# Late output-projection tiles: residual row loaded before the reciprocals, whose loads GpSimd issues

## The chip, the cores and the metric

The kernel runs on one core of a Trainium2 chip. The metric is the device time of one execution in microseconds (us); smaller is better. A core has five engines that work side by side, each through its own queue in order: TensorE (PE: matmuls and transposes, with its weight loads shown apart as PEld), VectorE (DVE), ScalarE (ACT), GpSimd (POOL) and SyncE (SP, which here only issues DMAs). POOL can issue DMAs too. An engine's instruction starts when the semaphores that it waits for have been raised by other engines or by DMAs that have landed.

## The reference

One step of a hybrid transformer with 1024 latent and 256 context tokens, D = 1024, two layers and a final RMSNorm. Layer 0 is gated attention with two mixers (A attends to all keys, B to a window with a sink logit), layer 1 is a Fourier mixer. The part around the change is the end of layer 0 and the beginning of layer 1:

```python
    # layer 0 (even), latents; the context tokens in the same way
    oa = dense_block_attention(qa, jnp.concatenate([ka, ka_ctx], axis=1), ...)
    ob = window_attention_with_ctx(qb, kb, vb, kb_ctx, vb_ctx, sink)
    yl = jnp.concatenate([oa * jax.nn.silu(ga), ob * jax.nn.silu(gb)], axis=-1) @ w_out
    xl = xl + gtl[:, None] * yl
    # layer 1 (odd)
    hl = modulate(rms_norm(xl, norm_g[l]), shl[:, None], scl[:, None])
    u, gate = jnp.split(hl @ w_in, 2, axis=-1)
    yl = (fourier_mix(u) * jax.nn.silu(gate)) @ w_out
```

## The kernel before

The tokens are ten tiles of 128 rows, r = 0 to 9 (8 and 9 are the context). All products of layer weights are made by `mm3` (L258): every float32 operand is split into a high and a low half in the PE's rounded float32 form, and a product is three matmuls (high by high, high by low, low by high; L265). A projection tile of 128x1024 outputs has two halves of 512 columns, 24 matmuls each.

**What is staged.** Attention runs in two sweeps over units (tile, head group, pair). `weigh` (L1040) makes the weighted values of a unit in PSUM (L1056); ACT copies its upper half out (L1065), DVE adds the lower half to it (L1067), and SP stores the result to `od` in DRAM (L1073). When a query tile is done, `totals` (L1021) takes the reciprocals of its softmax sums, transposes them (L1032), copies the row out on ACT (L1035), and SP stores it to `scd` in DRAM (L1037). The copies and sums of 64x256 and the rows of 16x128 share one pool of buffers, "e"; a buffer is free for its next user when the store that reads it has landed. The gates lie in `gd`.

**The output projection** is a filler: `proj_step` (L1325) of a tile is fed in between attention units, as soon as what it reads is finished, and the rest is drained when attention has ended (L1453). `proj_load` (L1316) calls `proj_in` (L1215), which loads a tile one or two tiles ahead (`load_to`, L1405):

- `ol`, the attention rows, from `od` (L1220), and `gl`, the gates, from `gd` (L1223);
- `rl`, the reciprocals, from `scd`: two loads, one for each mixer, each one row spread over 64 partitions (L1225, 64x1024, 256 KB);
- gates by reciprocals (L1226), by attention rows (L1227), both on POOL, and the split into high (L279) and low (L283) half;
- `xr`, the residual row, from the input (L1237), 128x1024.

`out_proj` (L1240) then makes both halves `oz` on PE, multiplies each by the layer's gate (L1248, DVE) and adds it to the residual row (L1249, DVE). `proj_step` stores the new row to `x1d` (L1348), squares it on ACT for the norm (L1349), and, when both tiles of a pair are done, makes 1/rms (`rsqrt`, with its power on POOL at L244), the pair's sum and difference (L1361 on ACT, L1362 and L1363 on DVE) and, with every second pair, four sums and differences of these (L1378, L1379, L1382, L1385, on DVE, with copies of one row on ACT). `quad_T` (L1279) transposes them on PE (`eoE`, `eoO`) for layer 1, between the halves of later tiles.

The pairs are (0,4), (2,6), (3,7), (1,5), (8,9), taken in that order. Tiles 0, 4, 2 and 6 are **early**: their loads are issued by POOL while attention runs (`ld`, L1216). Tiles 3, 7, 1, 5, 8 and 9 are **late**: attention's units have all been written (`late[0]`, L1451), and `ld` is SP. Their buffers come from the big zones `BIG` (`OB[0]`), handed out by `take` and returned by `drop`, and their PSUM banks from `next_bank` (L181), which goes round a ring of banks that includes the one in which the attention outputs are summed.

**What sets the order.** The kernel's text gives dependences and the sequence in which buffers are taken; a list scheduler with its own cost estimates then sets the order of each engine's queue, over the whole program. An edit in one place can so change the order on all engines from there on. DMAs issued by SP go round eight completion semaphores; a DMA waits for the one eight before it.

**Names in the orders below.** `oz_10502`/`oz_10530` are the halves of tile 7, `oz_10428`/`oz_10456` of tile 3, `oz_10666`/`oz_10694` of tile 5, `oz_10592`/`oz_10620` of tile 1. `av_30_10247` and `av_31_10267` are the last two attention units, whose sums are `e_10261` and `e_10281`; `e_10231` is the sum of the unit before, `e_10296` the last row of reciprocals. `p_10398` is the half of pair (2,6) that ACT makes, and `p_10403` the first of the four sums made from pairs (0,4) and (2,6); the three `eoE` transposes read it.

Of the kernel before, what the change touches and what calls it, by code (L numbers as in the profile page):

```python
# [17 lines left out]
P = 128  # L18
D = 1024
# [120 lines left out]
def hybrid_step(ctx: ExitStack, tc: tile.TileContext, I, O):  # L140
    nc = tc.nc
    pe, act, dve, pool, sp = nc.tensor, nc.scalar, nc.vector, nc.gpsimd, nc.sync
# [13 lines left out]
    def take(tag, shape, dt=F32):  # L156
        tags = (tag,) if isinstance(tag, str) else tag
        z = min((t for t in tags if spare[t]), key=lambda t: spare[t][0])
        i = spare[z].popleft()[1]
        size = 2 if dt == BF16 else 4  # L160
        for s in shape[1:]:
            size *= s
        assert size <= 4 * ZONES[z][1]
        made[0] += 1
        return Buf(z, i, up.tile(list(shape), dt, tag=f"{z}{i}", name=f"{z}{made[0]}", bufs=1))

    def drop(*bufs):
        for b in bufs:
            stamp[0] += 1
            spare[b.zone].append((stamp[0], b.idx))  # L170
# [22 lines left out]
    scd = dr.tile([NT, 2, 8, P], F32, name="scd")  # L193
# [76 lines left out]
    def pick(key, cycle):  # L270
        turn[key] = turn.get(key, -1) + 1
        return {"d": dve, "p": pool, "a": act}[cycle[turn[key] % len(cycle)]]
# [8 lines left out]
    def split(dst_h, dst_l, src, hc="a", lc="p"):  # L281
        copy("hi" + hc, hc, dst_h, src)
        pick("lo" + lc, lc).tensor_sub(dst_l, src, dst_h)  # L283
# [798 lines left out]
    def flush_held(n=0):  # L1082
        while len(held) > n:
            held.popleft()()
# [108 lines left out]
    OB, late = [("u", "w")], [False]  # L1193
# [21 lines left out]
    def proj_in(src, gate, r, resid):  # L1215
        ld = sp if gate is None or late[0] else pool  # L1216
        if gate is not None:
            flush_held()
            ol = take(OB[0], (P, 8, P))
            ld.dma_start(ol.a, src[r])  # L1220
            gl = take(OB[0], (P, 8, P))
            rl = take(OB[0], (P, 8, P))
            ld.dma_start(gl.a, gate[r])  # L1223
            for h in range(2):
                ld.dma_start(rl[64 * h : 64 * h + 64], scd[r, h].partition_broadcast(64))  # L1225
            pick("pm", XE["pm"]).tensor_mul(gl.a, gl.a, rl.a)  # L1226
            pick("pm", XE["pm"]).tensor_mul(ol.a, ol.a, gl.a)  # L1227
            drop(gl, rl)
        hi, lo = take(OB[0], (P, 8, P), F32R), take(OB[0], (P, 8, P), F32R)
        if gate is not None:  # L1230
            split(hi.a, lo.a, ol.a, "p" if late[0] else E_OH, E_OL)
            drop(ol)
        else:
            for c in range(2):
                split(hi[:, 4 * c : 4 * c + 4, :], lo[:, 4 * c : 4 * c + 4, :], src(c, r), "a", "d")
        xr = take(OB[0], (P, D))
        ld.dma_start(xr.a, resid[r * P : (r + 1) * P, :])  # L1237
        return hi, lo, xr

    def out_proj(name, r, ins, wo, gt, between=lambda h: None):  # L1240
        hi, lo, xr = ins
        for h in range(2):
            sl = slice(h * 512, h * 512 + 512)
            acc = next_bank(f"{name}{r}{h}") if late[0] else bank("g", f"{name}{r}{h}")
            mm3(acc, [(hi[:, k, :], lo[:, k, :], wo[k][0][:, sl], wo[k][1][:, sl]) for k in range(8)])
            between(h)
            yt = take("h", (P, 512))
            dve.tensor_mul(yt.a, acc, gt[:, sl])  # L1248
            pick("xa", XE["xa"]).tensor_add(xr[:, sl], xr[:, sl], yt.a)  # L1249
            drop(yt)  # L1250
        drop(hi, lo)
        return xr
# [63 lines left out]
    def proj_load(i, j):  # L1316
        r = pairs[i][j]
        v = r // 8
        if v not in gt0:
            gt0[v] = take(OB[0], (P, D))  # L1320
            sp.dma_start(gt0[v].a, gtd[0, v].partition_broadcast(P))
        ins[r] = proj_in(od, gd, r, I["xp"])
        return 0
# [459 lines left out]
    for g in range(4):  # L1783
# [34 lines left out]
        for r in (8, 9):  # L1818
            if AT_C[r - 8] == g:
                first[r] = proj_in(m1_at, None, r, x1d)  # L1820
# [7 lines left out]
    for r in (8, 9, 0, 1, 2, 3, 4, 5, 6, 7):  # L1828
        v = r // 8
        if v not in gt1:  # L1830
            gt1[v] = take(BIG, (P, D))
            sp.dma_start(gt1[v].a, gtd[1, v].partition_broadcast(P))
        ins1 = first.pop(r) if r in first else proj_in(m1_at, None, r, x1d)
        if r == 7:
            break
        xr = out_proj("of", r, ins1, wout1, gt1[v])
        yt = take(BIG, (P, D))
        ssq = sm.tile([P, 4], F32, tag="ssq", name=f"fss{r}")[:, 0:1]
        act.activation(yt.a, xr.a, AF.Square, accum_out=ssq)
        rs = rsqrt(f"frs{r}", ssq, 1, 1.0 / D, pw=PW[2])  # L1840
        dve.scalar_tensor_tensor(out=yt.a, in0=xr.a, scalar=rs[:, 0:1], in1=fg.a, op0=ALU.mult, op1=ALU.mult)
        sp.dma_start(O["y"][r * P : (r + 1) * P, :], yt.a)
        drop(xr, yt)


    hi, lo, xr = ins1
# [133 lines left out]
```

## Time and profile before

| what | us |
|---|---|
| median of 3 runs | 1191.29 |
| lowest and highest run | 1189.96, 1192.39 |
| the profiled execution | 1188.89 |
| its span, first to last instruction | 1187.1 |
| granted TensorE clock, mean of the span | 0.998 of full |

The page of the profile gives, for each engine, the time that it was busy, and groups of instructions by line. The timeline lists instructions in order of time: start, duration, engine, line, operation, output and inputs, count, and in brackets the idle time of the engine ahead of it with what ended it. A row with a count of several is a run of like instructions; matmuls overlap in the pipe, so that the distance between starts, not the printed duration, is what one costs. The tables of windows give each engine's busy time in a stretch, then the granted clock (PEclk), the busy share of the DMA engines and GB/s. The chain of waits goes back from the end of a stretch, at each step to what released it. Lines are those of the kernel before unless said otherwise; after the change the lines from L1225 on stand 3 or 4 higher.

### The profile page before, as it was taken

To read this page: it belongs to the slowest core of one execution; us is meant where nothing else is said; L and a number is where in the kernel's file an instruction comes from. 1 tells how busy PE (TensorE), PEld (TensorE's weight loads), DVE (VectorE), ACT (ScalarE), POOL (GpSimd) and SP (SyncE) were. 2 spreads that over 40 slices of the span, in tenths; PEclk is the share of its full clock that TensorE was granted. 3 is DMA by queue.
4 is the path that set the end of the run, shared out by engine and by line. 5 is a ranking of instruction groups with operands and counts; after the bars stand their busy time and mean duration, and the time that the engine had idled before them with its cause. 6 is when DMAs were issued, how large, how long until landed. Compare 5 with 4: busy or idle time off the path is not lost.

```text
span 1187.1 us, 22024 instructions
## 1 busy us (share of the span) xinstructions
PE 1150.7 (97%) x8103; PEld 1032.0 (87%) x8103; DVE 835.5 (70%) x1994; ACT 569.4 (48%) x1149; POOL 329.3 (28%) x294
## 2 busy tenths in 40 slices
PE   8999999999999999999999989999999999999997
PEld 6788899999999999899989887887877888998886
DVE  2489788877777776668888977876765962378543
ACT  4442455556656555556666674522363234342211
POOL 2355645512222221010110045275331226100001
PEclk9999999999999999999999999999999999999999
DMA  9978512323523232344352586785213426264321
GB/s 330 374 252 265 172 44 67 103 78 105 161 72 96 77 96 76 87 126 123 86 153 75 149 233 201 226 256 160 89 45 129 165 93 189 95 205 152 125 107 54
DMA packets 130096, 168.81 MB, mean 142 GB/s; under 512 B 26298, under 2 KB 86454, under 8 KB 129988
## 3 DMA queue, kind: packets, MB, share of 16 engines
q1 hardware_dynamic: 127476, 158.74, 43.4%
q0 software_dynamic: 2368, 8.39, 2.4%
q8 instruction: 64, 1.05, 0.4%
q14 instruction: 44, 0.36, 0.1%
q10 hardware_dynamic: 144, 0.26, 0.1%
HBM read 123.19 MB, written 44.16 MB: 141 GB/s over the span
## 4 chain that ended last, share of the span: by engine, by line
PE 76%; DMA 10%; DVE 6%; ACT 3%; issue 2%; SPq 2%; POOL 1%; POOLq 0%; DVEq 0%; ACTq 0%
PE of L265 9%; PE av L1056 9%; PE ga L265 8%; PE pt L1050 8%; PE q L265 8%; PE sL L933 5%; PE oz L265 4%; PE u L265 4%; PE g1O L265 4%; PE g1E L265 3%; PE kv L265 3%; PE sC L933 3%; PE g1c L265 2%; DMA od<-e 2%; DMA q<-qd 2%
## 5 line engine op out<-in xcount | busy, mean ns | idle before, releaser
L277 ACT ACTIVATE pt<-pt 128x512 fp32r<-128x512 f32 (+1 forms) x265 | 147.0, 576 | 107.6 <-PE pt L1050 60.3
L1053 DVE TENSOR_TENSOR pt<-pt,pt 128x512 fp32r<-128x512 f32 (+1 forms) x264 | 170.8, 658 | 37.9 <-ACT pt L277 37.0
L1056 PE MATMUL av<-pt,u 128*128 128x256 f32 x1008 | 167.0, 289 | 3.0 <-DVE e L1067 2.0
L1050 PE MATMUL pt<-identr,p 128*128 128x128 f32 x1008 | 156.9, 272 | 1.2 <-ACT p L974 0.8
L1056 PEld LDWEIGHTS av<-pt,u 128*128 128x128 f32 x1008 | 138.4, 189 | 7.1 <-DVE e L1067 2.6
L265 PE MATMUL q<-w,u 128*128 128x256 f32 x960 | 143.8, 287 | 0.0
L265 PEld LDWEIGHTS q<-w,u 128*128 128x128 f32 x960 | 126.9, 189 | 4.9 <-issue 0.8
L1050 PEld LDWEIGHTS pt<-identr,p 128*128 128x128 f32 x1008 | 119.3, 140 | 7.9 <-ACT p L974 1.0
L974 ACT ACTIVATE p<-p,nm 128x1280 f32<-128x1280 f32 (+1 forms) x80 | 95.5, 1194 | 62.3 <-DVE p L967 62.1
L265 PE MATMUL ga<-u,w 128*128 128x512 f32 (+1 forms) x576 | 124.4, 360 | 0.8 <-DVE byp L1029 0.5
L265 PEld LDWEIGHTS ga<-u,w 128*128 128x128 f32 x576 | 93.8, 188 | 15.0 <-ACT pt L277 1.2
L283 POOL TENSOR_TENSOR w<-h,w 128x512 fp32r<-128x512 f32 x38 | 51.1, 1363 | 143.5 <-DVE w L279 116.7
L933 PE MATMUL sL<-u,q 128*128 128x512 f32 x256 | 82.5, 411 | 1.4 <-DMA q<-qd 1.4
L974 ACT ACTIVATE p<-p,NM 128x640 f32<-128x640 f32 (+2 forms) x80 | 59.1, 739 | 38.1 <-DVE p L967 38.0
L933 PE MATMUL sC<-u,q 128*128 128x256 f32 x320 | 61.5, 293 | 2.3 <-DMA q<-qd 2.0
L967 DVE TENSOR_SCALAR_CACHE_REDUCE p<-sL 128x512 f32<-128x512 f32 x64 | 43.9, 685 | 23.5 <-PE sL L933 14.6
L967 DVE TENSOR_SCALAR_CACHE_REDUCE p<-sL,nm 128x512 f32<-128x512 f32 x64 | 47.7, 745 | 13.5 <-PE sL L933 12.6
L265 PE MATMUL oz<-u,w 128*128 128x512 f32 x192 | 56.9, 400 | 0.0
L707 POOL TENSOR_TENSOR h<-h,rope 128x512 f32<-128x512 f32 (+1 forms) x18 | 21.9, 1217 | 125.8 <-ACT h L790 80.0
L933 PEld LDWEIGHTS sC<-u,q 128*128 128x128 f32 x320 | 48.8, 189 | 6.4 <-DVE tot L1023 1.7
L265 PE MATMUL oz<-u,u 128*128 128x512 f32 x160 | 47.8, 402 | 4.3 <-DVE h L1248 2.4
L283 POOL TENSOR_TENSOR u<-h,u 128x512 fp32r<-128x512 f32 x16 | 21.1, 1325 | 108.6 <-ACT u L277 104.3
(728 smaller groups left out, 2590.1 us busy)
## 6 DMA issues: line engine op xcount, KB each, us to landing
q<-qd SPq DMA_DIRECT2D x80, 256.0 KB
h<-i_w_in SPq DMA_DIRECT2D x40, 256.0 KB
p<-i_ada_w SPq DMA_DIRECT2D x18, 512.0 KB
h<-i_w_out SPq DMA_DIRECT2D x32, 256.0 KB
pt<-i_ada_w SPq DMA_DIRECT2D x15, 512.0 KB
qd<-pt SPq DMA_DIRECT2D x20, 256.0 KB
q<-i_ada_w SPq DMA_DIRECT2D x9, 512.0 KB
qd<-q SPq DMA_DIRECT2D x18, 256.0 KB
```

The source lines that it names most:

```text
L265: pe.matmul(out, a, b, start=i == 0, stop=i == n - 1)
L277: act.activation(out, in_, AF.Copy)
L283: pick("lo" + lc, lc).tensor_sub(dst_l, src, dst_h)
L707: pick("rope", XE["rope"]).tensor_mul(t1.rearrange("p t h (b c) -> p t (h b) c", b=2), y.rearrange("p t h (b c) -> p t (h b) c", b=2), cb)
L933: pe.matmul(ps, q_at(q, s, hc), keys, start=s == 0, stop=s == 1)
L967: dve.tensor_scalar(p[i][:, end[i] : end[i] + n], ps, sign, last[i], op0=ALU.mult, op1=ALU.min, accum_out=c)
L974: act.activation(p[i][:, 0 : end[i]], p[i][:, 0 : end[i]], AF.Exp, bias=last[i], scale=-1.0, accum_out=SU[:, t, hd + i, 0:1],)
L1050: pe.transpose(tp[:, jj * 256 + i * P : jj * 256 + i * P + P], p[i][:, off : off + P], ident)
L1053: dve.tensor_sub(pt[:, 1, 0:n], tp[:, 0:n], pt[:, 0, 0:n])
L1056: pe.matmul(acc, vv, pt[:, s, jj * 256 : jj * 256 + 256], start=c + jj + s == 0, stop=c + jj == nt - 1 and s == 1,)
```

## The change

In `proj_in`, for tiles that are late, the residual row's buffer is taken, and its load issued by SP, right behind the load of the gates; the two loads of reciprocals are issued by POOL in place of SP. Early tiles have their loads in the order and on the queue that they had.

```diff
             gl = take(OB[0], (P, 8, P))
             rl = take(OB[0], (P, 8, P))
             ld.dma_start(gl.a, gate[r])
+            if late[0]:
+                xr = take(OB[0], (P, D))
+                sp.dma_start(xr.a, resid[r * P : (r + 1) * P, :])
             for h in range(2):
-                ld.dma_start(rl[64 * h : 64 * h + 64], scd[r, h].partition_broadcast(64))
+                pool.dma_start(rl[64 * h : 64 * h + 64], scd[r, h].partition_broadcast(64))
             pick("pm", XE["pm"]).tensor_mul(gl.a, gl.a, rl.a)
...
-        xr = take(OB[0], (P, D))
-        ld.dma_start(xr.a, resid[r * P : (r + 1) * P, :])
+        if gate is None or not late[0]:
+            xr = take(OB[0], (P, D))
+            ld.dma_start(xr.a, resid[r * P : (r + 1) * P, :])
         return hi, lo, xr
```

Six late tiles with two loads each: 12 DMA issues go from SP's queue to POOL's, and six loads of a residual row move ahead of the work on the gates. The buffers are taken in another sequence, too (tile 7's residual row is `pt_10328` before, `p_10320` now). No arithmetic is added or left out.

The scheduler's order is another one from there on. On PE, before, at the end of tile 7's second half and ahead of the first transposes, tile 5's first half stands around the last attention unit:

```order
L265 MATMUL oz_10530<-u_9276,q_10325 128x512
L265 MATMUL oz_10666<-u_8504,w_10496 128x512
L265 MATMUL oz_10666<-u_8505,w_10496 128x512
L1056 MATMUL av_31_10267<-pt_10273,u_7079 128x256 x4
L265 MATMUL oz_10666<-u_8504,u_10497 128x512
...
L265 MATMUL oz_10666<-u_9276,u_10497 128x512
L1279 MATMUL eoE_10820<-identr,p_10403 128x128
L1279 MATMUL eoE_10831<-identr,p_10403 128x128
L1279 MATMUL eoE_10844<-identr,p_10403 128x128
L265 MATMUL oz_10428<-u_8504,w_10309 128x512
```

And PE at the same place of the program now:

```order
L1056 MATMUL av_31_10267<-pt_10273,u_7079 128x256 x4
L265 MATMUL oz_10530<-u_8850,q_10326 128x512
...
L265 MATMUL oz_10530<-u_9276,pt_10327 128x512
L1283 MATMUL eoE_10820<-identr,p_10403 128x128
L1283 MATMUL eoE_10831<-identr,p_10403 128x128
L1283 MATMUL eoE_10844<-identr,p_10403 128x128
L265 MATMUL oz_10428<-u_8504,u_10311 128x512
...
L265 MATMUL oz_10428<-u_9276,w_10312 128x512
L265 MATMUL oz_10666<-u_8504,u_10498 128x512
```

The 24 matmuls of `oz_10666` stood between tile 7's last matmul and the transposes; they now stand behind the transposes and behind the 24 of `oz_10428`. The last attention unit stands 18 matmuls of tile 7 ahead of the transposes.

On ACT, the difference of the two orders around the last copies of attention (a row with - stands there before, with + now):

```order
 L1035 ACTIVATE e_10244<-tt_10242 16x128
+L1353 ACTIVATE h_10386,ss_104<-u_9925 128x1024
 L1065 ACTIVATE e_10230<-av_31_10217 64x256
-L1361 ACTIVATE p_10398<-u_9925,r11y 128x1024
+L1065 ACTIVATE e_10260<-av_30_10247 64x256
 L1035 ACTIVATE e_10296<-tt_10294 16x128
-L1065 ACTIVATE e_10260<-av_30_10247 64x256
+L1365 ACTIVATE p_10398<-u_9925,r11y 128x1024
 L1065 ACTIVATE e_10280<-av_31_10267 64x256
```

`p_10398` stood ahead of the last row of reciprocals (L1035) and now stands behind it; the copy of the last attention unit but one (L1065 `e_10260`) has moved ahead of both.

On SP, the difference around the store of the sum `e_10231`:

```order
-L1223 DMA q_10653<-gd 128x1024
-L1225 DMA u_10580<-scd 64x1024 x2
-L1237 DMA pt_10328<-i_xp 128x1024
-L1223 DMA u_10579<-gd 128x1024
+L1352 DMA x1d<-u_9925 128x1024
 L1073 DMA od<-e_10231 64x2x128
+L1226 DMA w_10492<-i_xp 128x1024
 L1037 DMA scd<-e_10296 16x127
```

Ahead of that store stood two loads of gates, two of reciprocals and tile 7's residual row; now there stands the store of tile 6's new row, and a residual row's load follows behind it.

## The prediction

> **What bounds the kernel now.** I read the page first, then the waits of PE in the stage that the change touches, then the chain of waits there, then the timelines of SP, DVE and ACT.
>
> ```profile
> span 1187.1 us, 22024 instructions
> PE 1150.7 (97%) x8103; PEld 1032.0 (87%) x8103; DVE 835.5 (70%) x1994; ACT 569.4 (48%) x1149; POOL 329.3 (28%) x294
> ```
>
> PE is busy for 97% of the span. An edit moves the end only by making PE's gaps shorter or longer, or its clock lower. The changed loads start at about 760 us (a row further below); the matmuls that use them, and the transposes behind them, lie between 783 and 880 us. There PE waits three times, of which two matter:
>
> ```profile
> PE oz L265 <- DVE u L283: 1.9, 1, 1.9
> PE av L1056 <- DVE e L1067: 1.0, 1, 1.0
> PE eoO L1279 <- DVE pt L1269: 0.3, 1, 0.3
> ```
>
> The two lie next to each other (PE's timeline: start, duration, instruction, count, idle time ahead with its releaser):
>
> ```profile
> 791.07 0.63 PE L1056 MATMUL av<-pt,u 128*128 128x256 f32 x4
> 791.54 0.27 PE L1032 MATMUL tt<-identr,byp 128*16 128x128 f32 x1
> ...
> 802.56 0.63 PE L265 MATMUL oz<-u,w 128*128 128x512 f32 x2
> 804.16 0.74 PE L1056 MATMUL av<-pt,u 128*128 128x256 f32 x4 [0.97 <-DVE e L1067]
> 806.77 0.79 PE L265 MATMUL oz<-u,u 128*128 128x512 f32 x1 [1.87 <-DVE u L283]
> ...
> 809.92 0.63 PE L265 MATMUL oz<-u,w 128*128 128x512 f32 x2
> ```
>
> The chain of waits (start, length, what) says whence the two waits come:
>
> ```profile
> 796.91 5.97 DMA od<-e
> ...
> 802.99 0.28 ACT e L1035
> ...
> 803.69 0.42 DVE e L1067
> 804.11 2.62 DVE u L283
> ...
> 813.58 0.33 PE eoE L1279 x3
> 813.91 11.11 PE oz L265 x48
> ```
>
> A store of an attention sum lands late; ACT's last row of reciprocals (L1035) waits for its buffer, and behind it in ACT's queue stands the copy that DVE's sum (L1067) needs.
>
> The gap has a tail, in the windows (us, busy time of PE, PEld, DVE, ACT and POOL, granted clock, DMA share, GB/s):
>
> ```profile
> 730.00:740.00 10.00, 7.55 (x41) 6.24 (x39) 9.90 (x24) 6.56 (x14) 5.48 (x6) 1.00 0.52 150
> 800.00:810.00 10.00, 7.16 (x26) 5.34 (x25) 8.20 (x8) 1.03 (x3) 4.69 (x4) 0.83 0.47 152
> ```
>
> The clock was 0.83 in that stretch. Seven matmuls start from 806.77 up to 809.92, so they took 3.15 us. At full clock one costs 0.23 (the chain's last row: 11.11 / 48 = 0.2315), seven 1.6: 1.5 lost. **The gap costs 0.97 + 1.87 + 1.5 = 4.35 us**, the most that the change can win here.
>
> Why did the store land late?
>
> ```profile
> 794.62 1.09 SPq L1225 DMA_DIRECT2D u<-scd  x2
> 795.81 0.54 SPq L1237 DMA_DIRECT2D pt<-i_xp  x1
> 796.43 0.39 SPq L1223 DMA_DIRECT2D u<-gd  x1
> 796.91 0.62 SPq L1073 DMA_DIRECT2D od<-e  x1
> ```
>
> ```profile
> 793.77 0.41 DVE L1067 TENSOR_TENSOR e<-av,e 64x256 f32<-64x256 f32 x1
> ...
> 801.53 0.69 DVE L1249 TENSOR_TENSOR pt<-pt,h 128x512 f32<-128x512 f32 x1 [4.12 <-DMA pt<-i_xp]
> 802.14 1.28 DVE L1362 SCALAR_TENSOR_TENSOR pt<-w,r11y,p 128x1024 f32<-128x1024 f32 x1
> ...
> 804.03 2.69 DVE L283 TENSOR_TENSOR u<-u,w 128x1024 fp32r<-128x1024 f32 x1
> 806.64 1.27 DVE L1363 SCALAR_TENSOR_TENSOR p<-w,r11y,p 128x1024 f32<-128x1024 f32 x1
> ...
> 812.08 0.41 DVE L1067 TENSOR_TENSOR e<-av,e 64x256 f32<-64x256 f32 x1
> 812.42 2.54 DVE L1249 TENSOR_TENSOR pt<-pt,h 128x512 f32<-128x512 f32 x1
> 814.88 1.21 DVE L1385 TENSOR_TENSOR p<-w,p 128x1024 f32<-128x1024 f32 x1
> ```
>
> The stored sum was ready at 793.77 + 0.41 = 794.18, but SP's queue held two loads of reciprocals, the residual row and a gate ahead of it: issued at 796.91. Just these issues the change takes away, and with them DVE's 4.12 us for the residual row.
>
> **The change part by part.** *What it takes off SP.* With only the store of tile 6's row ahead, which was ready long before, the store can go at about 794.3, 2.6 earlier. By the row's 5.97 it lands at 800.3. The residual row's wait of 4.12 ends 2.2 us before the other (802.22 against 804.11), so by itself it hardly moves PE; next behind it is ACT's L1035.
>
> *What it adds on POOL.*
>
> ```profile
> L1225 SPq DMA_DIRECT2D u<-scd x8: 450/480/590, 761.3 to 807.3; - x8
> L1225 POOL DMA_DIRECT2D u<-scd x4: 522/539/567, 695.3 to 737.7; - x4
> DMA to landing us min/median/max: 4.2/5.8/6.4
> DMA to landing us min/median/max: 3.6/8.0/11.8
> ```
>
> (The first landing line is that of the reciprocals, on either queue; the second that of the residual rows.) An issue costs 0.48 on SP and 0.54 on POOL: 12 x 0.48 = 5.8 us of SP's queue go, 12 x 0.54 = 6.5 us of POOL's come, 1.1 a tile. POOL's multiplies behind them start that much later. I cost this at nothing: tile 5's high half, which PE used at 802.56, is now used behind 24 matmuls of another tile, some 13 us later (sum below), and later tiles have more. Without that cover it is 1.1 us a tile, or what a late landing costs (rival C). The Trainium skill, page "SBUF — State Buffer", section "🔬 SBUF: two separate sides", speaks against this part: descriptors of a DMA issued from GpSimd's queue are written by GpSimd, which DVE can lock out, and a DMA of 620 ns took 3100. By that, as an estimate from the page, a load would be 2.5 us later, and with all of it on the path the time 2.5 us longer. The landings above, of loads from both queues, 4.2 to 6.4, show nothing of it.
>
> *What it moves.* PE's order loses the 24 matmuls of tile 5's first half ahead of the three transposes, 24 x 0.2315 = 5.6 us of cover. The transposes need the first quad sum (p_10403), and the 24 matmuls behind them a PSUM bank that the last attention sum (e_10281) empties. Both stand at the end of this chain: L1361, L1362, L1363, L1378, then e_10281. And ACT's part of it was early:
>
> ```profile
> 796.79 1.16 ACT L1361 ACTIVATE p<-u,r11y 128x1024 f32<-128x1024 f32 x1 [4.67 <-POOL r11y L244]
> 802.99 0.27 ACT L1035 ACTIVATE e<-tt 16x128 f32<-16x128 f32 x1 [5.04 <-DMA od<-e]
> ```
>
> Before, L1361 ran at 796.79, ahead of the row that waits for the store. Now it stands behind it. Two more rows, and then step by step:
>
> ```profile
> 814.99 1.06 ACT L1349 ACTIVATE h<-pt 128x1024 bf16<-128x1024 f32 x1 [2.88 <-DVE pt L1249]
> 732.89 2.33 PE L265 MATMUL oz<-u,u 128*128 128x512 f32 x9 [2.45 <-DVE h L1248]
> ```
>
> 1. PE has two matmuls of tile 5 less: after the row of 802.56 only the last attention unit's four (791.07 to 791.54: 0.47) remain to be placed earlier, so PE comes to the transposes at 802.56 + 0.47 = 803.03 and would be through at 803.36.
> 2. ACT: store landed at 800.3, L1035 0.27, L1361's successor from 800.6 to 801.8.
> 3. DVE: L1362 1.28, then the same six instructions as from 806.64 to 812.49: 5.85. e_10281 at 801.8 + 7.1 = 808.9.
> 4. A DVE operation with two inputs in SBUF that meets a multiply of POOL is stretched: the rows of 2.69 (1.21 for that shape in the row of 814.88) and 2.54 (0.69 in the row of 801.53) lose 1.5 and 1.85. Those six met none in their 5.85. It can now meet none to three of POOL's multiplies; I take one, 1.7, as in 804.03: e_10281 at 810.6.
> 5. PE stands idle for 810.6 - 803.36 = 7.2 us, in two pieces, at the transposes and at the half behind them. Should the last attention unit itself wait earlier, that comes off these pieces.
> 6. Then come 24 + 2 matmuls, 6.0 us, before tile 5's low half is needed. DVE has till then three operations of 0.69, two of 1.21 and ACT's square between (1.06): 5.55. No further wait; at the most the 1.87 of before.
>
> 7. The clock. The idle 2.84 of 803 to 807 cost 1.5 behind it; the idle 2.45 at 732.89 cost nothing (clock 1.00 in its window). A wait of 7.2 is beyond both; I take the nearer, 1.5, with 0 and two such tails, 3.0, as bounds. The Trainium skill, "TensorE: Matmul & The Clock Gate", gives half clock after an idle window of 3.4 us; with a wait of that length at each of two places it would be some 3.4 us of loss by the page, 1.9 more than my term, and no run here has yet shown a wait so long.
>
> **Sum**: 7.2 + 0 + 1.5 - 4.35 = +4.35 us. The profiled execution of 1188.89 would be 1193.2; it stands 2.4 below the median, and the difference on the median of 1191.29 gives **1195.6**. Nothing later gives it back: PE has no other wait but the one of 0.3 us until 880, and what follows is issued in PE's order.
>
> Bounds: the store could land as fast as the reciprocals' fastest load, 4.2; then, with no meeting and no tail, e_10281 is at 807.1 and the sum is 3.7 - 4.35 = -0.6. Upwards: three meetings (+3.4), the 1.87, two tails (+1.5): +11.1.
>
> **The rivals.**
>
> A. *The change does what it says*: the store, freed from SP's queue, lands within 2.4 us, and the chain is done before PE needs it. A store's landing is bounded below by this row of the chain at another place:
>
> ```profile
> 734.75 2.12 DMA scd<-e
> ```
>
> With 2.12 L1035 is through by 796.7, ACT's product is done at 798.0 (POOL's r11y of 796.79 is then as late), e_10281 at 805.1: idle 1.7, no tail, -2.6. With less, up to -4.35. That is **1186.9 to 1188.7**, faster. It decides as soon as the chain ends before 805.3. For it speaks that 2.7 of the store's lateness are SP's; against it that stores of this form took 5.97 here with the DMA engines half idle (0.47).
>
> B. *An equal wait takes the place of the one removed*: step 2 to 5 hold, but DVE meets no multiply and PE's clock does not fall. Then 5.5 - 4.35 = +1.2, and with a landing of 4.2 -0.6: **1190.7 to 1192.5**, no change. It decides where POOL's multiplies fall, which the issues on POOL move by 1.1 us a tile.
>
> C. *POOL's loads come late*: an issue on POOL waits, behind it its multiplies, and PE waits for tile 5's or tile 1's high half on top of the forecast. The worst landing of a residual row, 11.8, against the reciprocals' 5.8, is +6.0: with the sum **1201.6**. For it speaks that POOL's queue is in order, and that a load whose buffer is still in use holds all multiplies behind it; against it 4.2 to 6.4 in all landings so far.
>
> **How the numbers follow.** About 0.2%, 2.4 us, is what a measurement of this kernel can tell from no change. The forecast, slower by 2.4 to 11, gets 0.63: it rests on orders that are given, and on one stretched operation. A gets 0.12, B 0.17, C 0.08. So faster 0.12, same 0.17, slower 0.63 + 0.08 = 0.71. The range goes from B's and the bound's lower end, with a little of A, 1189.0, to the upper bound of the sum, 1191.29 + 11.1 = 1202.4; outside lie A and the worst of C, under 0.2.
>
> **What would show it.** In the changed kernel's timeline PE should wait at the transposes (L1283) for DVE's L1382 and at the next half for L1067, 7 us together, and the 0.97 and 1.87 should be gone. ACT's L1365 should start behind L1035 after 800 us. The store of e_10231 should be issued at about 794.3, and DVE should no longer wait for a residual row. The window of 800 to 820 should have a clock under 1. The prediction is wrong if the transposes wait for less than 2 us, if L1365 runs before 798, or if PE's waits are for POOL's halves (L279), not DVE's sums.

## The result, and the profile after

| | kernel before | changed kernel |
|---|---|---|
| median, us | 1190.93 (7 runs) | 1196.78 (7 runs) |
| lowest and highest run | 1187.80, 1192.39 | 1192.37, 1198.89 |
| ratio to the kernel before | | 1.0053, 95% interval 1.0038 to 1.0067 |
| span of the profiled execution | 1187.1 | 1192.6 |

The changed kernel is slower by 5.9 us; 4.35 were forecast, and the range holds the time. The waits of PE between 730 and 900 us are now two of a kind that the kernel before did not have:

```profile
PE eoE L1283 <- DVE p L1382: 4.8, 1, 4.8
PE oz L265 <- DVE e L1067: 3.6, 1, 3.6
```

PE's timeline shows them next to each other, at the three transposes and at tile 3's half behind them:

```profile
801.29 0.40 PE L265 MATMUL oz<-u,pt 128*128 128x512 f32 x1
806.50 0.90 PE L1283 MATMUL eoE<-identr,p 128*128 128x128 f32 x3 [4.81 <-DVE p L1382]
811.04 1.22 PE L265 MATMUL oz<-u,u 128*128 128x512 f32 x2 [3.64 <-DVE e L1067]
...
814.93 0.63 PE L265 MATMUL oz<-u,u 128*128 128x512 f32 x2
```

Together 8.45 us. And the clock stays low for longer than before (windows, columns as before; the last three are granted clock, DMA share, GB/s):

```profile
800.00:810.00 10.00, 2.59 (x11) 1.53 (x9) 10.00 (x5) 0.45 (x1) 8.44 (x7) 0.73 0.59 202
810.00:820.00 10.00, 8.96 (x31) 7.20 (x32) 8.11 (x11) 2.82 (x4) 4.75 (x3) 0.76 0.79 251
```

Nine matmuls start from 811.04 up to 814.93: 3.89 us where 9 x 0.2315 = 2.08 would do, 1.8 lost; the transposes took 0.90 for the 0.33 of before, 0.6 more. 8.45 + 1.8 + 0.6 - 4.35 of before = 6.5. That is 0.7 more than the stage measures below; 0.3 of it is the third wait of before (`eoO`), which is gone, and the rest isn't accounted for.

One profiled execution differs from the next in places that have nothing to do with the change, so a yardstick is needed that leaves them out. It is the length of the stage from the last transposes of reciprocals but one (L1032) to the first matmul of the context's part of layer 1 (`g1c`): up to a matmul or two it holds the same PE work in all kernels here. Before and after:

```profile
778.49 0.27 PE L1032 MATMUL tt<-identr,byp 128*16 128x128 f32 x1
...
889.05 0.50 PE L265 MATMUL g1c<-u,u 128*128 128x256 f32 x2 [0.44 <-ACT u L1268]
```

```profile
776.95 0.27 PE L1032 MATMUL tt<-identr,byp 128*16 128x128 f32 x1
...
893.28 0.50 PE L265 MATMUL g1c<-u,w 128*128 128x256 f32 x2 [0.44 <-ACT u L1272]
```

110.57 before, 116.33 after: +5.8, as much as the measured difference. Each is one execution. lock_probe (below) has the order of the kernel before up to the piece added behind it, and so gives that stage a second time: 111.23. What DVE did meanwhile:

```profile
789.00 0.42 DVE L1067 TENSOR_TENSOR e<-av,e 64x256 f32<-64x256 f32 x1 [0.89 <-ACT e L1065]
...
797.60 2.23 DVE L1366 SCALAR_TENSOR_TENSOR pt<-w,r11y,p 128x1024 f32<-128x1024 f32 x1 [2.34 <-ACT p L1365]
799.87 3.30 DVE L1367 SCALAR_TENSOR_TENSOR p<-w,r11y,p 128x1024 f32<-128x1024 f32 x1
803.09 3.36 DVE L1382 TENSOR_TENSOR p<-w,pt 128x1024 f32<-128x1024 f32 x1
...
806.97 2.55 DVE L1386 TENSOR_TENSOR pt<-w,p 128x1024 f32<-128x1024 f32 x1
...
810.58 0.41 DVE L1067 TENSOR_TENSOR e<-av,e 64x256 f32<-64x256 f32 x1
```

The chain that PE waits for starts at 797.60, earlier than forecast, and takes 13.4 us, longer than forecast: four of its operations last 11.4 us that took 1.28 + 1.27 + 1.21 + 1.45 = 5.2 before. GpSimd was at work beside each of them:

```profile
793.30 2.40 POOL L1229 TENSOR_TENSOR w<-w,q 128x1024 f32<-128x1024 f32 x1 [8.49 <-DMA w<-gd]
...
796.36 2.39 POOL L1229 TENSOR_TENSOR u<-u,u 128x1024 f32<-128x1024 f32 x1
798.72 3.37 POOL L1230 TENSOR_TENSOR u<-u,w 128x1024 f32<-128x1024 f32 x1
...
802.30 3.07 POOL L1230 TENSOR_TENSOR p<-p,u 128x1024 f32<-128x1024 f32 x1
...
806.41 1.05 POOL L279 CAST u<-u 128x1024 fp32r<-128x1024 f32 x1
807.39 1.05 POOL L279 CAST w<-p 128x1024 fp32r<-128x1024 f32 x1
```

The first of these rows says why its work lay there: GpSimd had stood still for 8.49 us, for a load of gates. SP issued that load at 783.32, and it landed 9.8 us later; why so late wasn't followed up.

ACT and SP, ahead of the chain:

```profile
794.43 0.38 ACT L1065 ACTIVATE e<-av 64x256 f32<-64x256 f32 x1 [5.47 <-DMA od<-e]
795.85 0.27 ACT L1035 ACTIVATE e<-tt 16x128 f32<-16x128 f32 x1 [1.04 <-DMA w<-i_xp]
796.41 1.15 ACT L1365 ACTIVATE p<-u,r11y 128x1024 f32<-128x1024 f32 x1 [0.29 <-POOL r11y L244]
```

```profile
789.44 0.58 SPq L1073 DMA_DIRECT2D od<-e  x1
```

The store of e_10231 goes out as soon as the sum is made (789.00 + 0.42), so SP's queue is no longer in its way, and DVE waits for no residual row. The change does what it says; what comes with it costs more. With the durations of before, the chain from 797.60 would have been done at 804.8, and PE, through with the transposes at 802.0, would have stood idle for some 2.8 us, about as long as the two waits that the change took away (0.97 + 1.87). This is an estimate, and no run tests it: none has the changed kernel's order without the longer operations.

### The profile page after: what moved, and what is told of

It reads as the page before. It is cut to its first block, busy times and chain, and to the rows that moved or that the text cites. A ratio compares the mean times of both kernels' runs of the same rounds, so it can differ in the third digit from the quotient of the medians.

```text
span 1192.6 us, 22027 instructions
## 1 busy us (share of the span) xinstructions
PE 1154.3 (97%) x8103; PEld 1035.5 (87%) x8103; DVE 840.2 (70%) x1994; ACT 570.2 (48%) x1149; POOL 336.2 (28%) x306
## 4 chain that ended last, share of the span: by engine, by line
PE 80%; DMA 7%; DVE 6%; issue 2%; ACT 2%; POOL 1%; SPq 1%; POOLq 0%; DVEq 0%; ACTq 0%
PE of L265 9%; PE ga L265 9%; PE av L1056 9%; PE pt L1050 8%; PE q L265 8%; PE oz L265 6%; PE sL L933 5%; PE u L265 4%; PE g1E L265 3%; PE g1O L265 3%; PE sC L933 3%; PE kv L265 3%; PE g1c L265 2%; DMA w<-gd 1%; PE sB L1005 1%
## 5 line engine op out<-in xcount | busy, mean ns | idle before, releaser
L283 POOL TENSOR_TENSOR w<-h,w 128x512 fp32r<-128x512 f32 x38 | 51.0, 1360 | 144.0 <-DVE w L279 117.2
L265 PE MATMUL oz<-u,u 128*128 128x512 f32 x224 | 63.6, 404 | 3.6 <-DVE e L1067 3.6
L967 DVE TENSOR_SCALAR_CACHE_REDUCE p<-sL,nm 128x512 f32<-128x512 f32 x64 | 47.7, 745 | 13.4 <-PE sL L933 12.5
L265 PEld LDWEIGHTS oz<-u,u 128*128 128x128 f32 x224 | 41.9, 192 | 13.1 <-DVE e L1067 4.0
L265 PE MATMUL oz<-u,w 128*128 128x512 f32 x176 | 52.9, 399 | 0.0
```

The lines of the kernel that those rows point to most:

```text
L265: pe.matmul(out, a, b, start=i == 0, stop=i == n - 1)
L967: dve.tensor_scalar(p[i][:, end[i] : end[i] + n], ps, sign, last[i], op0=ALU.mult, op1=ALU.min, accum_out=c)
```

## The experiments

Theories, as the expectations name them. **O**: the order counts; PE waits for what its new order puts next, and the queue on which a load is issued costs nothing. **D** is its sharper form: both waits stand at the end of one chain on DVE. **T**: the transposes stand too early, and that is all. **Q**: loads issued by GpSimd hold up its multiplies. **X**: the early residual rows cost. **L**: the reciprocals come sooner outside SP's queue, so that GpSimd's multiplies run beside DVE's chain. **K**: DVE and GpSimd shut each other out.

All kernels at a glance (ratio to the kernel before, measured alongside, with its interval; stage as above, from one profile of each kernel):

| kernel | residual row | reciprocals by | ratio (95%) | stage, us |
|---|---|---|---|---|
| before | last | SP | 1 | 110.57 |
| changed | early | GpSimd | 1.0053 (1.0038 to 1.0067) | 116.33 |
| xr_only | early | SP | 0.9979 (0.9964 to 0.9994) | 108.74 |
| pool_only | last | GpSimd | 1.0057 (1.0034 to 1.0079) | 115.34 |
| act_q | early | ScalarE | 0.9989 (0.9975 to 1.0003) | 107.58 |
| before_bare | last | SP | 1.0042 (1.0027 to 1.0058) | 114.84 |
| after_t81 | early | GpSimd | 1.0058 (1.0037 to 1.0079) | 116.34 |
| after_e | early | GpSimd | 1.0027 (1.0012 to 1.0043) | 113.91 |
| xr_e | early | SP | 0.9973 (0.9956 to 0.9991) | 108.92 |
| act_e | early | ScalarE | 0.9992 (0.9976 to 1.0009) | 110.33 |

**Each half of the change alone, and another queue.** xr_only is the changed kernel with

```diff
-                pool.dma_start(rl[64 * h : 64 * h + 64], scd[r, h].partition_broadcast(64))
+                ld.dma_start(rl[64 * h : 64 * h + 64], scd[r, h].partition_broadcast(64))
```

> One part alone: late residual rows are loaded early, the reciprocals' loads stay on SP. In its order the first transposes stand behind tile 8, 230 matmuls later than in the change. Theory O (PE waits for whatever DVE's chain its order puts next; the queue of the loads costs nothing): no wait at the transposes, a gap of at most the old 4.35 us, so 1187 to 1191 us and a ratio of 0.996 to 1.000. Theory Q (loads issued by GpSimd hold up its multiplies): no such loads, 1.000. Theory X (early residual rows cost, by their buffers and SP's queue): as slow as the change, 1.005.

Measured 1187.91 us, ratio 0.9979: faster, so X falls. There is no wait at the transposes; PE waits twice, as long as in the kernel before:

```profile
PE oz L265 <- DVE u L283: 1.9, 1, 1.9
PE av L1056 <- DVE e L1067: 0.9, 1, 0.9
```

pool_only is the kernel before with

```diff
-                ld.dma_start(rl[64 * h : 64 * h + 64], scd[r, h].partition_broadcast(64))
+                pool.dma_start(rl[64 * h : 64 * h + 64], scd[r, h].partition_broadcast(64))
```

> The other part alone: GpSimd issues the late reciprocals, the residual row is loaded last as before. In its order the transposes stand right behind tile 7's last matmul, as in the change. Theory O: PE waits at the transposes or at tile 3's half for the last attention sum, 3 us or more, ratio 1.002 to 1.006. Theory Q: 1.005, with waits of PE for GpSimd's halves. Theory X: 1.000.

Measured 1196.40 us, ratio 1.0057. This half alone gives all of the slowdown. Its waits and, on DVE, the longest operation of its chain:

```profile
PE eoE L1279 <- DVE p L1378: 3.0, 1, 3.0
PE oz L265 <- DVE e L1067: 2.8, 1, 2.8
PE av L1056 <- DVE e L1067: 1.4, 1, 1.4
```

```profile
804.91 4.77 DVE L1378 TENSOR_TENSOR p<-w,pt 128x1024 f32<-128x1024 f32 x1
```

PE waits for DVE's sums, as O has it; not once for a half that GpSimd makes, as Q would. act_q is the changed kernel with

```diff
-                pool.dma_start(rl[64 * h : 64 * h + 64], scd[r, h].partition_broadcast(64))
+                (act if late[0] else pool).dma_start(rl[64 * h : 64 * h + 64], scd[r, h].partition_broadcast(64))
```

> The change, but the late reciprocals are issued by ScalarE in place of GpSimd. PE's order from tile 7 on is that of xr_only, with the transposes behind tile 8. Theory O in its simple form: as xr_only, 0.996 to 1.000. Theory Q: as before, 1.000. Theory L (the reciprocals come sooner when they are not in SP's queue, so that GpSimd's multiplies run beside DVE's chain and stretch it): slow whatever PE's order, 1.003 to 1.006, with DVE operations of 2 to 3.4 us in the chain.

Measured 1189.01 us, ratio 0.9989. The waits:

```profile
PE oz L265 <- DVE pt L283: 1.3, 1, 1.3
PE oz L265 <- DVE u L283: 0.7, 1, 0.7
```

It too takes the reciprocals out of SP's queue, and is not slow. L forecast operations of 2 to 3.4 us in its chain, and they aren't there:

```profile
798.27 1.72 DVE L1366 SCALAR_TENSOR_TENSOR pt<-w,r11y,p 128x1024 f32<-128x1024 f32 x1
...
804.71 1.27 DVE L1367 SCALAR_TENSOR_TENSOR p<-w,r11y,p 128x1024 f32<-128x1024 f32 x1
805.91 1.22 DVE L1382 TENSOR_TENSOR p<-w,pt 128x1024 f32<-128x1024 f32 x1
```

So loads outside SP's queue don't by themselves bring GpSimd's work beside the chain, and this half of L falls. What a chain stretched by GpSimd costs, the other half, this run doesn't test. So far the slow kernels are those that have the transposes bare behind tile 7, and they are also those in which GpSimd issues; Q is not yet out.

**The order without the loads.** before_bare leaves every load where it was in the kernel before, and binds only PE's order:

```diff
+            if (r, h) == (5, 0):
+                for ins in mms[5, 0][:1]:
+                    tc.add_manual_dep(ins, mms[3, 0][-1].name, mybir.DependencyInfo(mybir.DependencyClass.NoSync, mybir.DependencyReason.SCHED_ONLY), reason="order")
```

(`mms[r, h]` are the matmuls of tile r's half h; an edge of this kind sets the order on PE and adds no wait. Up to 812 us the orders of DVE, ACT, GpSimd and SP are those of the kernel before.)

> The kernel before with all loads as they were; one constraint of order on PE alone puts tile 5's first half behind tile 3's, so that the transposes stand bare behind tile 7's last matmul, as in the change. Theory O: PE waits at the transposes for DVE's first quad sum and then for the last attention sum, 2 to 6 us more than before, ratio 1.002 to 1.005. Theories Q, X and L: the loads are those of before, 1.000.

Measured 1195.13 us, ratio 1.0042; O holds, Q, X and L would have had 1.000. PE waits

```profile
PE eoE L1283 <- DVE p L1382: 4.2, 1, 4.2
PE av L1057 <- DVE e L1068: 1.6, 1, 1.6
PE oz L265 <- DVE e L1068: 1.4, 1, 1.4
```

with no load moved. In this kernel the order alone costs 4.2 thousandths, 5 us. Its chain on DVE isn't stretched, but for a low half's L284 of 2.69 that stands in it as in the kernel before; it starts late, behind the wait for the residual row that the changed kernel no longer has:

```profile
804.15 0.69 DVE L1253 TENSOR_TENSOR pt<-pt,h 128x512 f32<-128x512 f32 x1 [4.24 <-DMA pt<-i_xp]
804.76 1.28 DVE L1366 SCALAR_TENSOR_TENSOR pt<-w,r11y,p 128x1024 f32<-128x1024 f32 x1
...
809.25 1.27 DVE L1367 SCALAR_TENSOR_TENSOR p<-w,r11y,p 128x1024 f32<-128x1024 f32 x1
810.45 1.21 DVE L1382 TENSOR_TENSOR p<-w,pt 128x1024 f32<-128x1024 f32 x1
```

So the same place of the transposes lays bare two different chains: here a late one of plain operations, in the changed kernel (and in pool_only) an early one that GpSimd stretches by some 6 us.

**Transposes, or DVE's chain?** after_t81 is the changed kernel in which PE's first transposes must come behind tile 8:

```diff
-            pe.transpose(tp[:, n * P : n * P + P], row[:, k * P : k * P + P], ident)
+            with tc.issue_after(ends[8, 1].ins) if key == "E" and k < 3 else nullcontext():
+                pe.transpose(tp[:, n * P : n * P + P], row[:, k * P : k * P + P], ident)
```

> The changed kernel with one constraint of order on PE: the first transposes come behind tile 8's last matmul. DVE's order up to the last attention sum (e_10281) is that of the change, with the chain of quad sums ahead of it. Theory D (PE waits for the end of DVE's chain, and tile 3's half waits there for the PSUM bank that e_10281 empties): the two waits of the change, 4.8 and 3.6 us, become one of 8 to 9.5 ahead of tile 3's half, and the time stays that of the change, ratio 1.004 to 1.006 to the kernel before. Theory T (the transposes stand too early, and that is all): their 4.8 us and part of the slow clock go, ratio 1.000 to 1.002.

Measured 1197.55 us, ratio 1.0058, and the stage as long as that of the changed kernel to 0.01 us, with the orders of DVE and GpSimd unchanged. T falls. The two waits have become one:

```profile
PE oz L265 <- DVE e L1068: 9.0, 1, 9.0
```

after_e leaves the transposes and puts the chain on DVE behind the last attention sum (`sums[-1]`):

```diff
-        dve.scalar_tensor_tensor(out=xe.a, in0=xa.a, scalar=rs[:, 0:1], in1=xo_.a, op0=ALU.mult, op1=ALU.add)
+        with tc.issue_after(sums[-1]) if i == 1 else nullcontext():
+            dve.scalar_tensor_tensor(out=xe.a, in0=xa.a, scalar=rs[:, 0:1], in1=xo_.a, op0=ALU.mult, op1=ALU.add)
```

> The changed kernel with one constraint of order on DVE: the last attention sum e_10281 comes ahead of the chain of quad sums. In its order tile 3's half follows tile 7's directly, then the transposes, then tile 5. Theory D: tile 3's half no longer waits, its 24 matmuls (5.6 us) run beside DVE's chain, and the transposes wait for less than 2 us; what is late next are tile 5's halves, whose high half GpSimd has ready at about 807.5 in the change and whose low half DVE makes behind its chain: 2 to 6 us of waiting there. Ratio 1.000 to 1.004, 1 to 6 us faster than the change. Theory T: the transposes still wait 4 us or more, with little change of the time, 1.004 to 1.006.

Measured 1193.93 us, ratio 1.0027: 2.4 us of the stage come back. The waits are as D foresaw, the next one being tile 5's low half, which DVE makes behind its chain:

```profile
PE oz L265 <- DVE u L283: 4.7, 1, 4.7
PE eoE L1284 <- DVE p L1384: 1.5, 1, 1.5
```

So it isn't one instruction that stands wrongly. DVE has some 13 us of work there, of which about 6 are the stretch, and what PE does meanwhile must not need it.

**Why the chain took 13 us.** lock_probe adds a piece behind the end of the kernel before, in which DVE and GpSimd run on buffers of their own: six additions alone, six beside four multiplies, eight from PSUM beside four multiplies, six beside four casts, four multiplies alone.

```diff
+            if name == "mul" or name == "psum":
+                pool.tensor_mul(go.a, ga_.a, gb_.a)
+            if name == "cast":
+                pool.tensor_copy(gr.a, ga_.a)
...
+            if name == "psum":
+                dve.tensor_add(vo[:, 0:512], vp, vb[:, 0:512])
+            else:
+                dve.tensor_add(vo.a, va.a, vb.a)
```

> The kernel before, with a piece added behind its end that measures one thing by itself: DVE additions of 128x1024 with both inputs in SBUF, first alone, then beside GpSimd multiplies of 128x1024, then 128x512 additions with one input in PSUM beside such multiplies, then the first kind beside GpSimd casts; at the end the multiplies alone. Theory K (the two engines shut each other out): alone 1.21 and 2.40; beside each other they take turns, so that the DVE operations that meet a multiply last 2 to 3.7 us and the multiplies beside them grow too, while the additions from PSUM keep 0.68 and the multiplies beside those 2.40. Rival (a shared bandwidth): every operation of both engines grows by one factor. Rival (no interplay; the long operations in the change have another cause): 1.21, 0.68 and 2.40 throughout.

Its time, 1252.98 us, is that of the added piece. The five parts as windows (us, then busy time and count of PE, PEld, DVE, ACT, POOL):

```profile
1195.30:1202.90 7.60, 0.00 (x0) 0.00 (x0) 7.35 (x6) 0.00 (x0) 0.00 (x0) 0.50 0.00 0
1202.90:1218.70 15.80, 0.00 (x0) 0.00 (x0) 15.44 (x6) 0.00 (x0) 13.00 (x4) 0.50 0.00 0
1218.70:1228.50 9.80, 0.00 (x0) 0.00 (x0) 5.53 (x8) 0.00 (x0) 9.39 (x4) 0.50 0.00 0
1228.50:1239.00 10.50, 0.00 (x0) 0.00 (x0) 10.22 (x6) 0.00 (x0) 7.85 (x4) 0.50 0.00 0
1239.00:1249.00 10.00, 0.00 (x0) 0.00 (x0) 0.00 (x0) 0.00 (x0) 9.36 (x4) 0.50 0.00 1
```

Alone an addition takes 7.35 / 6 = 1.23, a multiply 9.36 / 4 = 2.34. Beside each other the two need 15.4 together, not far from the 7.35 + 9.36 = 16.7 that one after the other would need: they take turns. The first addition, which begins just ahead of the first multiply, keeps its 1.23; the next four last 3.25 each, and the multiplies 3.2 to 3.4. From PSUM an addition keeps its 0.69, and the multiplies beside it their 2.35. Beside GpSimd's casts, too, the four additions in the middle grow, to 1.94. K holds. A shared bandwidth would, by its forecast, have made all operations grow by one factor; the additions grew 2.6-fold, the multiplies 1.4-fold, and the additions from PSUM not at all. The Trainium skill, page "SBUF — State Buffer", section "Who interferes with whom", says the same: an operation of DVE with two inputs in SBUF contends with one of GpSimd that reads SBUF, and the port pair that they contend for is an exclusive lock.

The Trainium skill, page "SBUF — State Buffer", section "🔬 SBUF: two separate sides", says that a load issued by GpSimd can starve while DVE runs an operation in a mode that takes both ports. This change shows nothing of it. The view of the changed kernel's reciprocals is this:

```profile
DMA to landing us min/median/max: 3.4/5.1/9.7
```

It holds only loads that GpSimd issued, here all 20. The line of before, 4.2/5.8/6.4, is that of the eight early ones alone, which GpSimd issued there too. The twelve late ones can be read from their semaphores, each raised 16 times for one load: issued by SP before they landed in 3.3 to 8.9 us (median 4.2) and in xr_only in 4.8 to 7.6 (6.3); issued by GpSimd in 3.4 to 9.7 (5.2) in the changed kernel and in 3.4 to 7.8 (5.4) in pool_only. The gates' load from SP's queue that took 9.8 was issued within 0.1 us of the one that took 9.7.

**A version that beats both.** xr_e is xr_only with the constraint of after_e, act_e is act_q with it.

> xr_only (residual rows early, reciprocals on SP) with the constraint of after_e: the last attention sum and the low halves of tiles 1 and 5 stand ahead of DVE's chain of quad sums, and the transposes behind tiles 1, 3 and 5. Theory D: what PE waited for in xr_only, 0.9 us for the attention sum and 1.9 for tile 1's low half, shrinks, since DVE comes to that half without the chain ahead of it; no wait over 1.5 us in the stage, 0 to 2 us less than xr_only, ratio 0.996 to 0.998. If the chain, moved back, is then late for tile 8 or 9: a wait there of 1 to 3 us and no gain over xr_only, 0.998 to 1.000.

Measured 1186.64 us, ratio 0.9973: faster than both kernels of the study, but not to be told from xr_only, and its stage is no shorter (108.92 for 108.74). The wait for the attention sum is gone, others of 1.7, 0.6 and 0.5 have come, the first a little over the 1.5 that D allowed. The two longest:

```profile
PE oz L265 <- DVE pt L283: 1.7, 1, 1.7
PE eoE L1284 <- DVE u L1274: 0.6, 1, 0.6
```

> act_q (residual rows early, late reciprocals issued by ScalarE) with the same constraint. Theory D: of the 1.3 and 0.7 us that PE waited for low halves in act_q the second goes; the time is that of act_q within 1 us, ratio 0.996 to 0.999. If ScalarE's queue, where an issue that waits stands ahead of copies, is the bound: a wait of PE for ScalarE or for DVE's attention sums of over 2 us, 0.999 or more.

Measured 1188.26 us, ratio 0.9992, stage 110.33: slower in its stage than act_q by 2.8, against what D led me to expect. PE waited four times for low halves that DVE made, 3.7 us in all for 2.0 in act_q, and not for ScalarE; why they were later than in act_q wasn't followed up.

## Why the prediction was right, point by point

- *What bounds*: PE's gaps. Right; the stage differs by 5.8, the time by 5.9.
- *Issues on GpSimd cost nothing by themselves*: PE never waited for a half made by GpSimd, in the changed kernel or in pool_only. That the 24 matmuls of another tile cover the later high half held. Rival C, late loads, didn't cost PE anything, though two late loads took 9.0 and 9.7. My reading that loads from both queues land in 4.2 to 6.4 was wrong: that line held none of SP's, and of SP's late ones three took over 7. That such loads cost nothing in an order that hides DVE's chain is not shown: GpSimd-issued loads with act_q's order weren't tried.
- *Step 1, PE at the transposes at 803.03*: it was through with tile 7 by 801.7, in an execution that was 1.5 earlier already at the last transposes but one (776.95 for 778.49). Right.
- *Step 2, ACT's product from 800.6*: it ran from 796.41, 4.2 us earlier, or 2.7 counted from those transposes. The path was right: the store of e_10231 took 6.3 us to land (5.97 forecast), at 795.78, and L1035 began at 795.85. The view names a residual row's load as what L1035 waited for, but that load's semaphore was raised for the last time at 796.99, after L1035 had begun. What failed is the time of the sum. I let it be ready at 794.18, as before; it was made at 789.00. Before, its copy on ACT had waited 2.57 us for a load (the row below), and now it didn't. GpSimd's 1/rms then came 0.3 behind L1035. L1365 before 798 is what I had named as a sign that the prediction is wrong, and yet the waits came out.

```profile
791.74 0.38 ACT L1065 ACTIVATE e<-av 64x256 f32<-64x256 f32 x1 [2.57 <-DMA u<-i_xp]
```

- *Step 4, one meeting with GpSimd, 1.7*: the mis-sized term. Four operations of the chain met GpSimd, and by the durations of before they lost 0.95 + 2.03 + 2.15 + 1.10 = 6.2; I had one meeting as the likeliest and three as the bound. The chain began 4.2 us earlier and lost 4.5 more, and e_10281 was done at 810.99, forecast 810.6. Counted from the transposes of step 1 it began 2.7 earlier and ended 1.9 late, which is most of what step 5 is short of. That the two errors nearly cancel is luck. A chain as early as this with one meeting of 1.7 would have ended at 806.5, and PE would have been idle for some 4.5 us: by the terms of the sum 4.5 + 1.5 - 4.35 = +1.6 us, an estimate, and less than the 2.4 at which the forecast of a slower kernel begins.
- *Step 5, idle 7.2*: 8.45. *Step 6, no further wait*: right. *Step 7, slow clock 1.5*: 1.8 at the matmuls and 0.6 at the transposes. By the windows the clock was at half speed for (0.27 + 0.24) x 10 / 0.5 = 10 us. The Trainium skill, "TensorE: Matmul & The Clock Gate", section "What's actually happening", has half clock come after an idle window of some 3.4 us. Three such windows fit the 10 us.
- *Rivals A and B* needed a chain done before 805.3, or one that meets no multiply and a clock that doesn't fall. The chain ended at 810.99, with four meetings, and the clock fell. That the residual row's wait was not what bound is shown by before_bare, where it stays (4.24), and by the changed kernel, where it is gone: both are slow, by 5 and 6 us.

Left open: xr_only is faster than the kernel before, by 1.8 us in its stage, with waits as long as before. Some 1.5 of it is the clock, which fell to 0.83 in the stage of before and stayed at 1.00 in that of xr_only. In these two executions that hangs on where the waits lie. In each trace here the granted clock changes only at times that are multiples of 3.41 us apart (before at 806.49 and 809.90, changed at 804.55 and 814.79, xr_only at 711.21 and 714.63). Cut into such intervals, both waits of before, 2.56 us of idle time, fall into the one from 803.1 to 806.5, and the next one is at half clock. In xr_only a boundary at 806.8 parts them into 0.94 and 1.85, and the clock stays. The wait of 2.45 at 732.89, which cost nothing in step 7, is parted at 731.4 into 1.0 and 1.5. Why the medians differ by 2.4 us, over 12 and 29 runs, is not explained by one execution of each.

## What to carry to other kernels

Where a scheduler sets the order, a DMA that changes queue is an edit of every engine's order: compare the orders before the times, and ask of the critical engine which work now stands ahead of what the others are still making. Cover is counted in matmuls between a producer's chain and its first reader; 24 of them, 5.6 us, moved to the other side here, and in before_bare that was worth 5 us without any load moved. When a chain of two-input DVE operations is about to be exposed, count the GpSimd work that can run beside it and add it in full: the two take turns.

## What the runs showed that I had not expected

How complete the exclusion is: 15.4 us for six additions beside four multiplies where in turn they would need 16.7, while additions that read PSUM lost nothing. In the kernel this turns a chain of 1.2 us steps into one of 2.2 to 4.8, and with one multiply after the other queued on GpSimd, one DVE step after the other meets the next one. And PE's wait of 2.45 us at 732.89, ahead of the first row in which the orders differ, is absent from the changed kernel's execution. For 1.4 of it the traces show one more such meeting. Before, GpSimd's multiply (727.61) began ahead of DVE's L283 (728.47), which stands ahead of PE's producer in DVE's order, and L283 took 2.61. In the changed kernel's execution L283 (728.01) began ahead of the multiply (728.32): it took 1.20, and the multiply 3.17. Whichever began first kept its time. What makes up the rest of the wait wasn't followed up.
